# A w_out stage of Winograd type: block sums formed by transfers into DRAM, one load a piece, products one at a time

## The chip, the cores and the metric

The kernel runs on one core of a Trainium2 chip. The metric is the device time of one execution in microseconds (us); given is the median of several runs. Engines are named as in the profile: PE (TensorE matmul), PEld (its weight loads), DVE (VectorE), ACT (ScalarE), POOL (GpSimd), SP (SyncE, which here issues most transfers).

## The reference

One layer on x of 512 tokens by 2048 channels, in float32. The part around the change:

```python
h = rmsnorm(x, g_pre[i])
proj = h @ w_in[i]
...
y_a = o_a @ w_br_a[i]            # branch A: gated DeltaNet
...
y_b = u @ w_br_b[i]              # branch B: convolution, layernorm, swish
gate_a, gate_b = jnp.split(jax.nn.sigmoid(gate_logits + b_gate[i]), N_BRANCHES, axis=-1)
mixed = (gate_a * y_a + gate_b * y_b) @ w_out[i]
x = x + rmsnorm(mixed, g_post[i])
e = p[i] @ w_ple_proj[i]
x = x + rmsnorm(jax.nn.sigmoid(x @ w_ple_gate[i]) * e, g_ple[i])
```

w_out is 2048 by 2048.

## The kernel before

**Precision.** Every large product runs in three passes: each operand is split into a rounded high part and the rest (a cast on ACT, a subtraction on DVE), and three matmuls add high·high, high·low and low·high.

**The stages ahead.** `gemm_cm` makes 128 output channels by 512 tokens from 48 matmuls; its weight tiles of 512 KB are loaded by SP (L122) and split by ACT L127 and DVE L128. It writes one of two PSUM banks of the pool `gps`. After each matmul `tick()` is called: generators that were put in by `spawn(gen, period)` go one step each `period` ticks, so side work is strewn between the matmuls in program order. Branch A's output product (`w_br_a`), the gates (`gate_a`, activation L716), and branch B's convolution (`dwconv`, DVE L689, POOL L693 and L695) interleave so. Branch B's product comes last; its evacuation is DVE L840 (times the gate) and L842 (added to `mixed`). `split_mixed` then makes the operands of the w_out stage out of `mixed`: quadrant A11, the sums S1 to S4, and A12, A22 (L872 to L890; splits by ACT L856 and DVE L858).

**The w_out stage.** The product of two 2 × 2 block matrices is done with seven block products in place of eight, once for each half `jp` of the output columns. With T1 = b11 + b12, T2 = T1 + b22, T3 = b12 + b22 and T4 = T2 + b21 (signs are in the stored blocks), the seven are P1 (A11 by b11), P2 (A12 by b21), P3 (S4 by b22), Q5 (S1 by T1), P6 (S2 by T2), P7 (S3 by T3) and Q4 (A22 by T4). Each product goes over four pieces `q`; a piece is one [128, 1024] block of w_out or of a sum, split by ACT L1037 and DVE L1038 into `wsp` tiles and used by twelve matmuls (L1061 to L1063) into two PSUM banks of 512 columns. That makes 7 × 4 × 2 = 56 pieces.

**Where pieces come from, before.** A table of entries (`e_a`, `e_b`, `e_c`, `e_63`, ...) says which blocks a piece needs. `load` (L978) has three `raw` buffers and, for each fourth load, one buffer `rw`. T1 is formed by a DVE add of two loaded blocks into a tile `t` (L993, four tiles). T2 and T4 are formed by accumulating transfers issued on POOL (`acc`, L985) into the same tile, T3 by a DVE add in place (L1002). So an entry holds one or two loads, an add or an accumulation, and one to three pieces. `next_piece_sw` keeps three or four pieces split ahead of PE and at most two sources loaded ahead of the split.

**Order and banks.** `run(products)` goes through q and, inside, through its products, so products run in pairs or threes: (P1, Q5), (P6, P7, P3), (P2, Q4) for the first half, and (P1, Q5), (P6, P3), (P2), (P7), (Q4) for the second. While the first runs, `stepper` calls the rest of `split_mixed` and `split_s3`. The pool `gps` is closed ahead of the stage and `fps` takes all eight PSUM banks. The products' sums and squares, and x reloaded from DRAM (`xr`, L1127, on SP), make x1; `post` scales it (L1134) by the row factors (`inv_rms`, DVE L957 and L958, POOL L960) and transposes it on PE (L1140). `gemm_tm` with w_ple_gate follows (L1219 to L1221), its weights again by L122, L127 and L128. SP, DVE, ACT and POOL each work off their instructions in order; the compiler's scheduling fixed that order.

Of the kernel before, what the change touches and what calls it, by code (L numbers as in the profile page):

```python
# [82 lines left out]
def _body(ctx, tc, A, out):  # L83
# [636 lines left out]
    def gate_a(i):  # L720
        gemm_cm(w_in_tile(GATE_TILE0 + i), hT, evac_gate(mixed, i, i))
# [205 lines left out]
    run_jobs()  # L927
    lnp_ctx.close()
    s2_ctx.close()
    gps_ctx.close()  # L930

# [4 lines left out]


    s3 = ctx.enter_context(tc.tile_pool(name="s3", bufs=20))  # L940
    fps = ctx.enter_context(tc.tile_pool(name="fps", bufs=8, space=PSUM))
    fsm = ctx.enter_context(tc.tile_pool(name="fsm", bufs=1))
    LOW, HIGH, ALL = (0, 1), (2, 3), (0, 1, 2, 3)
    SLOT, HP_, S3_ = (slots, "s"), (hpool, "h"), (s3, "s3")
# [16 lines left out]
        return r  # L961


    WO = A["w_out"]
    B11, B12, B22, B21 = range(4)
    entries = deque()
    sources = deque()
    pieces = deque()
    tb = {}
    count = [0]  # L970

    def load(jp, blk, q):
        loads[0] += 1
        if early[0] or loads[0] % 4:
            raw = rawp.tile([P, 1024], F32, tag="raw", name="raw", bufs=3)
        else:
            raw = s3.tile([P, 1024], F32, tag="rw", name="rw", bufs=1)
        nc.sync.dma_start(raw, WO[jp, blk, q])  # L978
        return raw

    early = [True]
    loads = [0]

    def acc(t, jp, blk, q):
        nc.gpsimd.dma_start(t, WO[jp, blk, q], accum_op=ALU.add)  # L985

    def e_a(jp, q):
        early[0] = jp == 0
        b11 = load(jp, B11, q)
        b12 = load(jp, B12, q)  # L990
        early[0] = False
        t = tb[q] = s3.tile([P, 1024], F32, tag="t", name="t", bufs=4)
        nc.vector.tensor_tensor(t, b11, b12, ALU.add)  # L993
        return [b11, t]

    def e_63(jp, q):
        acc(tb[q], jp, B22, q)
        return [tb[q], load(jp, B22, q)]

    def sum_t3(jp, q, b22):  # L1000
        b12 = load(jp, B12, q)
        nc.vector.tensor_tensor(b12, b12, b22, ALU.add)  # L1002
        return b12

    def e_b(jp, q):
        acc(tb[q], jp, B22, q)
        b22 = load(jp, B22, q)
        return [tb[q], sum_t3(jp, q, b22), b22]

    def e_p7(jp, q):  # L1010
        return [sum_t3(jp, q, load(jp, B22, q))]

    def e_p2(jp, q):
        acc(tb[q], jp, B21, q)
        return [load(jp, B21, q)]

    def e_t(jp, q):
        return [tb[q]]

    def e_c(jp, q):  # L1020
        return e_p2(jp, q) + [tb[q]]
# [27 lines left out]
    OPND = {"P1": "A11", "Q5": "S1", "P7": "S3", "P6": "S2", "P3": "S4", "P2": "A12", "Q4": "A22"}  # L1049

    def stage(entry, jp):
        for q in range(4):
            entries.append(lambda q=q: entry(jp, q))

    def mms(ps, pr, piece, q, t):
        wh, wl = piece
        for n in range(2):
# [4 lines left out]
            mm(ps, lh, wl[:, c], start=False, stop=False)  # L1062
            mm(ps, ll, wh[:, c], start=False, stop=kk == 7)  # L1063

    def bank():
        return fps.tile([P, T], F32, tag="f", name="f")

    def run(products, side=None):
        ps = {}
        for q in range(4):  # L1070
            for pr in products:
                piece = next_piece_sw()
                if q == 0:
                    ps[pr] = [bank() for _ in range(2)]
                for t in range(2):
# [54 lines left out]
    def post(tts, xr):  # L1130
        rm = inv_rms(ssm[:, tts[0]:tts[0] + 2, :], f"m{tts[0]}")
        for j in range(4):
            for n, tt in enumerate(tts):
                nc.vector.scalar_tensor_tensor(x1[tt][j], x1[tt][j], rm[:, n:n + 1], xr.pop((tt, j)), ALU.mult, ALU.add)  # L1134
            yield
            for k2 in (2 * j, 2 * j + 1):
                ps = fps.tile([P, T], F32, tag="f", name="x1t")
                for n in range(4):
                    k = 2 * k2 + n // 2
                    nc.tensor.transpose(ps[:, n * P:(n + 1) * P], x1[tts[n % 2]][j][:, (k % 4) * P:(k % 4 + 1) * P], ident)  # L1140
                xh = unit(HP_, "xh", F32R)
                nc.scalar.copy(xh, ps)
                xl = unit(HP_, "xl", F32R)
                nc.vector.tensor_tensor(xl, ps, xh.bitcast(F32), ALU.subtract)
                x1T[k2, tts[0] // 2] = (xh, xl)
                yield

    def stepper(gen, n=1):
        def f(k=None):
            for _ in range(n):  # L1150
                next(gen, None)
        return f
# [2 lines left out]
        for _ in gen:  # L1155
            pass

    for e, jp in ((e_a, 0), (e_b, 0), (e_c, 0), (e_a, 1), (e_63, 1), (e_p2, 1), (e_p7, 1), (e_t, 1)):
        stage(e, jp)
# [9 lines left out]
    s5 = [snap(S3_, x) for x in ps["Q5"]]  # L1169
    gp = [bcast_row(A["g_post"], j) for j in (0, 1)]  # L1170
    fin = out_fin(0, gp)
    ps = run(("P6", "P7", "P3"))
    u2 = [add(unit(S3_, "u2"), ps["P6"][t], s1[t]) for t in range(2)]
    d = [minus(unit(S3_, "d"), s5[t], u2[t]) for t in range(2)]
    u3 = [add(u2[t], ps["P7"][t], u2[t]) for t in range(2)]
    for t in range(2):
        fin(t, 1, add(d[t], ps["P3"][t], d[t]))
        fin(2 + t, 1, minus(s5[t], s5[t], u3[t]))
    ps = run(("P2", "Q4"))
    for t in range(2):  # L1180
# [185 lines left out]
```

## Time and profile before

| | |
|---|---|
| median of 3 runs | 2506.57 us (2505.82 to 2507.11) |
| profiled execution | 2508.75 us, span 2507.0 us |
| granted PE clock over the span | 0.998 |
| branch A's output product with gates and convolution | about 985 to 1480 us |
| w_out stage, first matmul to x1's last transposes | about 2144 to 2330 us |
| HBM read, written | 262.66 MB, 14.68 MB |

All times of the profile are from the start of the span of that one execution. "Busy" is the time in which an engine executes instructions; a bracket behind an instruction gives the idle time before it and what ended it. A window row gives busy time and number of instructions for each engine, the granted clock, the share of the 16 DMA engines and the rate. Line numbers in the profile are those of the code printed above; in the new kernel the lines of the stage lie a little elsewhere.

### The profile page before, as it was taken

What the parts mean: (1) busy time and instruction counts of PE and PEld (TensorE: products, weight loads), DVE (VectorE), ACT (ScalarE), POOL (GpSimd) and SP (SyncE); (2) the same over time, 40 slices, a digit from 0 to 9 for tenths busy, and PEclk for the clock granted to TensorE, in tenths of its full rate; (3) what the DMA queues carried; (4) which work ended last, traced back from release to release, by engine and by line L of the source; (5) the groups of instructions that cost most, each with busy time, mean ns of one, the idle gap of its engine ahead of it and who ended that gap; (6) DMA issues with size and microseconds to landing.
All of it is one profiled execution on the core that took longest, in us unless ns stands there. A gap on an engine that the chain in (4) does not pass through costs nothing.

```text
span 2507.0 us, 32580 instructions
## 1 busy us (share of the span) xinstructions
PE 2475.4 (99%) x12202; PEld 2040.6 (81%) x12202; DVE 1654.4 (66%) x3092; ACT 1053.9 (42%) x2083; POOL 134.6 (5%) x151
## 2 busy tenths in 40 slices
PE   8999999999999999999999999999999999998998
PEld 7888888888888888888888888888888888786886
DVE  6776767767676766887877869947323336667644
ACT  6555555565645555322222222235322224444532
POOL 0100000010000000000000000011000000100000
PEclk9999999999999999999999999999999999999999
DMA  6322222222122222323232333422222222676542
GB/s 257 117 96 72 85 80 85 81 76 89 67 92 79 84 85 76 109 97 109 97 109 97 102 105 110 165 87 101 101 96 97 98 96 99 190 228 197 200 170 76
DMA packets 85406, 279.45 MB, mean 111 GB/s; under 512 B 9472, under 2 KB 9728, under 8 KB 85248
## 3 DMA queue, kind: packets, MB, share of 16 engines
q1 hardware_dynamic: 81792, 266.89, 30.6%
q0 software_dynamic: 2304, 8.39, 1.8%
q10 hardware_dynamic: 1152, 2.10, 0.3%
q8 instruction: 95, 1.56, 0.2%
q14 instruction: 63, 0.52, 0.1%
HBM read 262.66 MB, written 14.68 MB: 111 GB/s over the span
## 4 chain that ended last, share of the span: by engine, by line
PE 94%; DMA 2%; DVE 2%; issue 1%; ACT 1%; POOL 0%; SPq 0%; DVEq 0%; POOLq 0%; ACTq 0%
PE g L184 25%; PE g L186 25%; PE g L182 25%; PE f L1221 2%; PE f L1219 2%; PE f L1220 2%; DMA raw<-in_w_out 1%; PE psB L468 1%; PE f L1062 1%; PE f L1063 1%; PE f L1061 1%; PE psS L474 1%; PE psA L462 1%; PE pg L569 1%; PE f L1296 0%
## 5 line engine op out<-in xcount | busy, mean ns | idle before, releaser
L186 PE MATMUL g<-hh,w 128*128 128x512 f32 x2320 | 916.0, 395 | 1.6 <-DVE w L128 1.6
L184 PE MATMUL g<-hl,w 128*128 128x512 f32 x2320 | 916.6, 395 | 0.0
L182 PE MATMUL g<-hh,w 128*128 128x512 f32 x2320 | 913.8, 394 | 0.0
L127 ACT CAST w<-raw 128x512 fp32r<-128x512 f32 x780 | 478.1, 619 | 867.1 <-PE g L186 760.0
L128 DVE TENSOR_TENSOR w<-raw,w 128x512 fp32r<-128x512 f32 x780 | 551.2, 711 | 433.4 <-ACT w L127 431.3
L186 PEld LDWEIGHTS g<-hh,w 128*128 128x128 f32 x2320 | 436.6, 188 | 88.7 <-DVE w L128 4.7
L184 PEld LDWEIGHTS g<-hl,w 128*128 128x128 f32 x2320 | 436.4, 188 | 86.2 <-issue 1.6
L182 PEld LDWEIGHTS g<-hh,w 128*128 128x128 f32 x2320 | 436.7, 188 | 84.2 <-issue 0.2
L689 DVE SCALAR_TENSOR_TENSOR uc<-sg,vec,uc 128x511 f32<-128x511 f32 (+14 forms) x480 | 351.3, 734 | 14.0 <-ACT uc L686 3.9
L410 DVE SCALAR_TENSOR_TENSOR cv<-g,vec,cv 128x511 f32<-128x511 f32 x144 | 106.3, 738 | 31.2 <-ACT cv L408 30.9
L184 PE MATMUL g<-ul,w 128*128 128x512 f32 x256 | 99.7, 390 | 0.0
L184 PE MATMUL g<-ol,w 128*128 128x512 f32 x256 | 99.7, 390 | 0.0
L186 PE MATMUL g<-oh,w 128*128 128x512 f32 x256 | 99.7, 389 | 0.0
L182 PE MATMUL g<-oh,w 128*128 128x512 f32 x256 | 99.7, 389 | 0.0
L182 PE MATMUL g<-uh,w 128*128 128x512 f32 x256 | 99.7, 389 | 0.0
L186 PE MATMUL g<-uh,w 128*128 128x512 f32 x256 | 99.7, 389 | 0.0
L604 DVE TENSOR_TENSOR prod<-UT,VT 128x2 f32<-128x2 f32 (+30 forms) x248 | 87.1, 351 | 6.6
L1061 PE MATMUL f<-wsp,oph 128*128 128x512 f32 x192 | 76.3, 401 | 6.2 <-ACT wsp L1037 6.1
L1062 PE MATMUL f<-wsp,oph 128*128 128x512 f32 x192 | 76.9, 401 | 2.7 <-DVE wsp L1038 2.6
L1220 PE MATMUL f<-w,xh 128*128 128x512 f32 x192 | 75.0, 391 | 2.1 <-DVE w L128 1.9
L1063 PE MATMUL f<-wsp,opl 128*128 128x512 f32 x192 | 75.6, 395 | 0.0
L1221 PE MATMUL f<-w,xl 128*128 128x512 f32 x192 | 75.0, 391 | 0.0
(298 smaller groups left out, 2666.5 us busy)
## 6 DMA issues: line engine op xcount, KB each, us to landing
raw<-in_w_in SPq DMA_DIRECT2D x290, 512.0 KB, 3.2
raw<-in_w_ple_gate SPq DMA_DIRECT2D x40, 512.0 KB, 4.2
raw<-in_w_out SPq DMA_DIRECT2D x35, 512.0 KB, 5.4
raw<-in_w_br_a SPq DMA_DIRECT2D x32, 512.0 KB, 3.3
raw<-in_w_br_b SPq DMA_DIRECT2D x32, 512.0 KB, 3.2
t<-in_w_out POOLq DMA_DIRECT2D x16, 512.0 KB, 8.3
rw<-in_w_out SPq DMA_DIRECT2D x9, 512.0 KB, 4.7
x<-in_x SPq DMA_DIRECT2D x8, 512.0 KB, 9.4
```

Of the source, the lines that this page charges most:

```text
L127: nc.scalar.copy(hi, rq)
L128: nc.vector.tensor_tensor(lo, rq, hi.bitcast(F32), ALU.subtract)
L182: mm(ps, wh, rh, start=(k == 0), stop=False)
L184: mm(ps, wh, rl, start=False, stop=False)
L186: mm(ps, wl, rh, start=False, stop=(k == NK - 1))
L410: nc.vector.scalar_tensor_tensor(y[:, s:], ps[:, 0:T - s], vv(w0 + 3 - s), y[:, s:], ALU.mult, ALU.add)
L689: nc.vector.scalar_tensor_tensor(y[:, s:], u[:, 0:T - s], vv(w0 + TAPS - 1 - s), y[:, s:], ALU.mult, ALU.add)
L1061: mm(ps, lh, wh[:, c], start=kk == 0, stop=False)
L1062: mm(ps, lh, wl[:, c], start=False, stop=False)
L1063: mm(ps, ll, wh[:, c], start=False, stop=kk == 7)
L1220: mm(ps[tt], lh, wl, start=False, stop=False)
L1221: mm(ps[tt], ll, wh, start=False, stop=k == NK - 1)
```

## The change

1. A generator `presum` is put in after `finish("oa")` in branch A, with a period of ten ticks. For each of the eight (jp, q) it has POOL issue 20 transfers of [128, 512] (256 KB): four plain loads and eight accumulating loads of w_out blocks into four tiles of the pool `slots`, and eight stores that put T1, T3, T2 and T4 into a DRAM tensor `wo_sums`. Ahead of the stores of T2 and of T4 it waits 24 ticks. That is 160 transfers, 42 MB. The four tiles come out of the tiles that gates and convolution use too.
2. In the stage every piece is one load by SP (now L1015), from w_out or from `wo_sums`. The DVE adds L993 and L1002 and the accumulating transfers L985 are gone. There are three `raw` and five `rw` buffers, in a cycle of eight loads (the first three loads take `raw`); up to five sources are loaded ahead of the split, and each split is followed by one more load.
3. Products run one at a time: P1, P2, Q5, P6, P3, P7, Q4 for the first half, P1, Q5, P6, P3, P2, P7, Q4 for the second. The side work during the first P1 goes four steps a piece in place of two.
4. `gps` stays open; `fps` has six banks, and `bank()` takes them in turn with the two of `gps`. x1's transposes take their bank there too.

```diff
-    gps_ctx = ExitStack()
-    gps = gps_ctx.enter_context(tc.tile_pool(name="gps", bufs=2, space=PSUM, side="right"))
+    gps = ctx.enter_context(tc.tile_pool(name="gps", bufs=2, space=PSUM, side="right"))
...
+    sums = dram.tile([2, 4, 4, P, 1024], F32, name="wo_sums")
+
+    def presum():
+        for jp in range(2):
+            for q in range(4):
+                cs = [slice(n * T, n * T + T) for n in range(2)]
+                a = [slots.tile([P, T], F32, tag="s", name="wsum") for n in range(2)]
+
+                def take(t, blk, add):
+                    for n in range(2):
+                        nc.gpsimd.dma_start(t[n], WO[jp, blk, q][:, cs[n]], **(dict(accum_op=ALU.add) if add else {}))
+                        yield
+
+                def give(t, m):
+                    for n in range(2):
+                        nc.gpsimd.dma_start(sums[jp, m, q][:, cs[n]], t[n])
+                        yield
+                yield from take(a, B11, False)
+                b = [slots.tile([P, T], F32, tag="s", name="wsum") for n in range(2)]
+                yield from take(b, B12, False)
+                yield from take(a, B12, True)
+                yield from take(b, B22, True)
+                yield from give(a, T1)
+                yield from give(b, T3)
+                yield from take(a, B22, True)
+                yield 24
+                yield from give(a, T2)
+                yield from take(a, B21, True)
+                yield 24
+                yield from give(a, T4)
+
     jobs.append(lambda: finish("oa"))
+    jobs.append(lambda: spawn(presum(), 10, "presum"))
...
-    gps_ctx.close()
...
-    fps = ctx.enter_context(tc.tile_pool(name="fps", bufs=8, space=PSUM))
+    fps = ctx.enter_context(tc.tile_pool(name="fps", bufs=6, space=PSUM))
...
+    WHICH = {"P1": (WO, B11), "P2": (WO, B21), "P3": (WO, B22),
+             "Q5": (sums, T1), "P6": (sums, T2), "P7": (sums, T3), "Q4": (sums, T4)}
-    def load(jp, blk, q):
+    def load(jp, pr, q):
+        n = loads[0]
         loads[0] += 1
-        if early[0] or loads[0] % 4:
+        if n < 3 or n % 8 in (1, 4, 7):
             raw = rawp.tile([P, 1024], F32, tag="raw", name="raw", bufs=3)
         else:
-            raw = s3.tile([P, 1024], F32, tag="rw", name="rw", bufs=1)
+            raw = s3.tile([P, 1024], F32, tag="rw", name="rw", bufs=5)
...
     def next_piece_sw():
-        ahead = 3 if count[0] < 10 else 4
-        while len(pieces) < ahead and (sources or entries):
-            while len(sources) < 2 and entries:
-                sources.extend(entries.popleft()())
+        while len(sources) < 5 and entries:
+            load(*entries.popleft())
+        while len(pieces) < (3 if count[0] < 10 else 4) and sources:
             split_piece()
+            if entries:
+                load(*entries.popleft())
         return pieces.popleft()
...
     gen = opening()
-    ps = run(("P1", "Q5"), stepper(gen, 2))
+    ps = run(("P1",), stepper(gen, 4))
     drain(gen)
...
+    ps = run(("P2",))
+    for t in range(2):
+        fin(t, 0, add(unit(S3_, "c11"), ps["P2"][t], s1[t]))
+    ps = run(("Q5",))
```

**How the order moves, first place: SP at the opening of the stage.** Rows are SP's transfers in its order; raw and rw are buffers, their numbers tell the tiles apart. Before:

```order
L978 DMA raw_17493<-in_w_out 128x1024
L978 DMA raw_17495<-in_w_out 128x1024
L978 DMA raw_17503<-in_w_out 128x1024
L978 DMA rw_17725<-in_w_out 128x1024
L978 DMA raw_17505<-in_w_out 128x1024
L978 DMA raw_17538<-in_w_out 128x1024
L978 DMA raw_17540<-in_w_out 128x1024
```

Now (pieces 0, 1, 2, 4, 7, 3, 5, 6 and 8):

```order
L1015 DMA raw_17685<-in_w_out 128x1024
L1015 DMA raw_17687<-in_w_out 128x1024
L1015 DMA raw_17689<-in_w_out 128x1024
L1015 DMA raw_17693<-in_w_out 128x1024
L1015 DMA raw_17711<-in_w_out 128x1024
L1015 DMA rw_17691<-in_w_out 128x1024
L1015 DMA rw_17699<-in_w_out 128x1024
L1015 DMA rw_17705<-in_w_out 128x1024
L1015 DMA rw_17750<-wo_sums_9445 128x1024
```

Five loads into raw tiles now stand ahead of the first rw load, in place of three; four rw loads follow it, where before raw loads did. raw_17711 takes the tile of raw_17687 and waits for that one's split.

**Second place: DVE at the opening.** gt are the gated outputs of branch B, sf and opl the stage's operands, wsp the split pieces. Before:

```order
L1038 TENSOR_TENSOR wsp_17500<-raw_17493,wsp_17499 128x1024
L840 TENSOR_TENSOR gt_16964<-g_17418,gt_16964 128x512
L842 TENSOR_TENSOR gt_12906<-gt_12906,gt_16964 128x512
L993 TENSOR_TENSOR t_17497<-raw_17493,raw_17495 128x1024
L1038 TENSOR_TENSOR wsp_17514<-raw_17503,wsp_17513 128x1024
L872 TENSOR_TENSOR sf_17362<-gt_10506,gt_12906 128x256
L1038 TENSOR_TENSOR wsp_17510<-t_17497,wsp_17509 128x1024
L858 TENSOR_TENSOR opl_17536<-sf_17362,oph_17534 128x512
L858 TENSOR_TENSOR opl_17626<-sf_17079,oph_17624 128x512
L993 TENSOR_TENSOR t_17507<-raw_17503,raw_17505 128x1024
```

Now (the last gate operation is L877, the split L1033; ahead of these rows stand, in this order, the split of piece 0, L875 and the split of piece 1):

```order
L877 TENSOR_TENSOR gt_13099<-gt_13099,gt_17157 128x512
L907 TENSOR_TENSOR sf_17555<-gt_10553,gt_13099 128x256
L1033 TENSOR_TENSOR wsp_17708<-raw_17689,wsp_17707 128x1024
L893 TENSOR_TENSOR opl_17732<-sf_17555,oph_17730 128x512
L893 TENSOR_TENSOR opl_17778<-sf_17272,oph_17776 128x512
L918 TENSOR_TENSOR sf_17555<-sf_17555,gt_10239 128x256
L918 TENSOR_TENSOR sf_17555<-sf_17555,gt_10553 128x256
L921 TENSOR_TENSOR sf_17735<-gt_12787,sf_17555 128x256
L921 TENSOR_TENSOR sf_17735<-gt_13099,sf_17555 128x256
L893 TENSOR_TENSOR opl_17770<-gt_12787,oph_17768 128x512
L893 TENSOR_TENSOR opl_17744<-sf_17555,oph_17742 128x512
L1033 TENSOR_TENSOR wsp_17747<-rw_17691,wsp_17746 128x1024
```

The sums L993 are gone, and the subtraction of piece 3 (wsp_17747) comes after those of pieces 1 and 2 and after the operand work.

**Third place: SP where x is loaded again, in the second half.** xr are the x tiles. Before:

```order
L1127 DMA xr_18302<-in_x 128x512
L978 DMA raw_18221<-in_w_out 128x1024
L1127 DMA xr_18304<-in_x 128x512
L1127 DMA xr_18306<-in_x 128x512
L978 DMA raw_18256<-in_w_out 128x1024
L1127 DMA xr_18308<-in_x 128x512
```

Now:

```order
L1122 DMA xr_18492<-in_x 128x512
L1122 DMA xr_18494<-in_x 128x512
L1122 DMA xr_18496<-in_x 128x512
L1015 DMA rw_18418<-in_w_out 128x1024
L1015 DMA raw_18438<-in_w_out 128x1024
L1122 DMA xr_18498<-in_x 128x512
L1122 DMA xr_18500<-in_x 128x512
```

The eight x loads stand in groups of two and three with two w_out loads between, in place of one w_out load each.

More of the change, by code (lines that the diff above doesn't have):

```diff
@@ L752, in evac_ya @@
         return f
+    WO = A["w_out"]
+    B11, B12, B22, B21 = range(4)
+    T1, T2, T3, T4 = range(4)
+    sums = dram.tile([2, 4, 4, P, 1024], F32, name="wo_sums")
[25 more added lines that the diff above has]
+                yield from give(a, T4)
     gate_a(4)
@@ L961, in inv_rms @@
         return r
-    WO = A["w_out"]
-    B11, B12, B22, B21 = range(4)
+    OPND = {"P1": "A11", "Q5": "S1", "P7": "S3", "P6": "S2", "P3": "S4", "P2": "A12", "Q4": "A22"}
+    WHICH = {"P1": (WO, B11), "P2": (WO, B21), "P3": (WO, B22),
+             "Q5": (sums, T1), "P6": (sums, T2), "P7": (sums, T3), "Q4": (sums, T4)}
     entries = deque()
@@ L968, in _body @@
     pieces = deque()
-    tb = {}
     count = [0]
-    def load(jp, blk, q):
+    loads = [0]
+    def load(jp, pr, q):
+        n = loads[0]
         loads[0] += 1
-        if early[0] or loads[0] % 4:
+        if n < 3 or n % 8 in (1, 4, 7):
             raw = rawp.tile([P, 1024], F32, tag="raw", name="raw", bufs=3)
         else:
-            raw = s3.tile([P, 1024], F32, tag="rw", name="rw", bufs=1)
[L978 to L1021, printed above, removed]
+            raw = s3.tile([P, 1024], F32, tag="rw", name="rw", bufs=5)
+        src, blk = WHICH[pr]
+        nc.sync.dma_start(raw, src[jp, blk, q])
+        sources.append(raw)
     def split_piece():
@@ L1063, in mms @@
             mm(ps, ll, wh[:, c], start=False, stop=kk == 7)
+    banks = [0]
     def bank():
-        return fps.tile([P, T], F32, tag="f", name="f")
+        banks[0] += 1
+        if banks[0] % 8 < 6:
+            return fps.tile([P, T], F32, tag="f", name="f")
+        return gps.tile([P, T], F32, tag="g", name="f")
     def run(products, side=None):
@@ L1136, in post @@
             for k2 in (2 * j, 2 * j + 1):
-                ps = fps.tile([P, T], F32, tag="f", name="x1t")
+                ps = bank()
                 for n in range(4):
@@ L1156, in drain @@
             pass
-    for e, jp in ((e_a, 0), (e_b, 0), (e_c, 0), (e_a, 1), (e_63, 1), (e_p2, 1), (e_p7, 1), (e_t, 1)):
-        stage(e, jp)
+    for jp, prs in ((0, ("P1", "P2", "Q5", "P6", "P3", "P7", "Q4")), (1, ("P1", "Q5", "P6", "P3", "P2", "P7", "Q4"))):
+        entries.extend((jp, pr, q) for pr in prs for q in range(4))
     def opening():
@@ L1165, in _body @@
     gen = opening()
-    ps = run(("P1", "Q5"), stepper(gen, 2))
+    ps = run(("P1",), stepper(gen, 4))
     drain(gen)
     s1 = [snap(S3_, x) for x in ps["P1"]]
-    s5 = [snap(S3_, x) for x in ps["Q5"]]
     gp = [bcast_row(A["g_post"], j) for j in (0, 1)]
     fin = out_fin(0, gp)
-    ps = run(("P6", "P7", "P3"))
-    u2 = [add(unit(S3_, "u2"), ps["P6"][t], s1[t]) for t in range(2)]
+    ps = run(("P2",))
+    for t in range(2):
+        fin(t, 0, add(unit(S3_, "c11"), ps["P2"][t], s1[t]))
+    ps = run(("Q5",))
+    s5 = [snap(S3_, x) for x in ps["Q5"]]
+    ps = run(("P6",))
+    u2 = [add(s1[t], ps["P6"][t], s1[t]) for t in range(2)]
     d = [minus(unit(S3_, "d"), s5[t], u2[t]) for t in range(2)]
+    ps = run(("P3",))
+    for t in range(2):
+        fin(t, 1, add(d[t], ps["P3"][t], d[t]))
+    ps = run(("P7",))
     u3 = [add(u2[t], ps["P7"][t], u2[t]) for t in range(2)]
     for t in range(2):
-        fin(t, 1, add(d[t], ps["P3"][t], d[t]))
         fin(2 + t, 1, minus(s5[t], s5[t], u3[t]))
-    ps = run(("P2", "Q4"))
-    for t in range(2):
-        fin(t, 0, add(s1[t], ps["P2"][t], s1[t]))
+    ps = run(("Q4",))
     for t in range(2):
         fin(2 + t, 0, add(u3[t], ps["Q4"][t], u3[t]))
-    ps = run(("P1", "Q5"))
+    ps = run(("P1",))
     s1 = [snap(SLOT, x) for x in ps["P1"]]
-    s5 = [snap(SLOT, x) for x in ps["Q5"]]
     gp = [bcast_row(A["g_post"], j) for j in (2, 3)]
     fin = out_fin(1, gp)
+    ps = run(("Q5",))
+    s5 = [snap(SLOT, x) for x in ps["Q5"]]
     xr = load_x_again(LOW, HP_)
-    ps = run(("P6", "P3"))
+    ps = run(("P6",))
     u2 = [add(unit(SLOT, "u2"), ps["P6"][t], s1[t]) for t in range(2)]
+    d = [minus(unit(SLOT, "d"), s5[t], u2[t]) for t in range(2)]
+    ps = run(("P3",))
     for t in range(2):
-        d = minus(unit(SLOT, "d"), s5[t], u2[t])
-        fin(t, 1, add(d, ps["P3"][t], d))
+        fin(t, 1, add(d[t], ps["P3"][t], d[t]))
     ps = run(("P2",))
@@ L1240, in hold @@
         if k < 14:
-            pool, tag, bufs = (s3, "t", 4) if k < 4 else (s3, "rw", 1) if k < 5 else (s3, "wx", 5) if k < 10 else (ring, "w", 4)
+            pool, tag, bufs = (s3, "rw", 5) if k < 5 else (s3, "wx", 5) if k < 10 else (ring, "w", 4)
             w = pool.tile([P, 1024], F32R, tag=tag, name="wh", bufs=bufs)
```

6 lines of the change are left out of this document (1 added, 5 removed).

## The prediction

> **What bounds the kernel now.** The page's first part says which engine to watch.
>
> ```profile
> PE 2475.4 (99%) x12202; PEld 2040.6 (81%) x12202; DVE 1654.4 (66%) x3092; ACT 1053.9 (42%) x2083; POOL 134.6 (5%) x151
> ```
>
> TensorE is busy for 2475.4 of 2507.0 us of span, and the change leaves the number of matmuls alone. So it can win only idle time of PE and time at a lower clock, and can lose only by making PE wait. Next, the busy time by windows: branch A, where the transfers are added, and then those 10 us windows of the w_out stage in which PE isn't full. Columns: window, its length, PE, PEld, DVE, ACT and POOL busy, the granted clock, the DMA share, GB/s.
>
> ```profile
> 985.00:1480.00 495.00, 495.00 (x2185) 410.14 (x2184) 396.94 (x580) 143.38 (x233) 14.04 (x11) 1.00 0.30 103
> 2140.00:2150.00 10.00, 9.12 (x41) 7.28 (x40) 6.26 (x8) 4.19 (x6) 0.33 (x1) 1.00 0.33 115
> 2150.00:2160.00 10.00, 8.74 (x37) 6.42 (x35) 7.47 (x12) 3.71 (x5) 1.60 (x2) 1.00 0.97 249
> 2160.00:2170.00 10.00, 7.17 (x29) 5.13 (x29) 8.00 (x10) 5.20 (x8) 1.75 (x2) 1.00 0.87 257
> 2260.00:2270.00 10.00, 8.07 (x28) 6.06 (x27) 6.20 (x6) 5.26 (x6) 1.74 (x2) 0.83 0.60 141
> 2280.00:2290.00 10.00, 9.58 (x42) 7.36 (x40) 6.89 (x9) 3.33 (x7) 0.00 (x0) 1.00 0.89 310
> 2290.00:2300.00 10.00, 7.25 (x33) 5.47 (x34) 8.38 (x12) 5.43 (x7) 0.73 (x1) 1.00 0.93 319
> 2310.00:2320.00 10.00, 8.07 (x44) 6.44 (x42) 9.55 (x17) 4.66 (x11) 0.00 (x0) 1.00 0.04 15
> 2320.00:2330.00 10.00, 9.44 (x48) 7.20 (x47) 9.38 (x18) 5.00 (x10) 1.20 (x1) 1.00 0.69 227
> 2330.00:2340.00 10.00, 10.00 (x53) 8.32 (x53) 9.43 (x16) 5.77 (x11) 0.00 (x0) 1.00 0.93 332
> ```
>
> Ten minus the PE column is the loss: 0.88 + 1.26 + 2.83 = 4.97 us at the opening, 1.93 in the 2260s, 0.42 + 2.75 = 3.17 in 2280:2300, 1.93 + 0.56 = 2.49 at the end of the last product. Together 12.56 us. The last row is a control: 332 GB/s, and PE is full. The waits of PE over the stage say for whom it stood still.
>
> ```profile
> PE f L1061 <- ACT wsp L1037: 6.1, 5, 1.5
> PE f L1062 <- DVE wsp L1038: 2.6, 3, 1.2
> PE f L1220 <- DVE w L128: 1.9, 1, 1.9
> PE x1t L1140 <- DVE snap L1134: 0.4, 1, 0.4
> ```
>
> 8.7 us are waits for the split of a w_out piece. The chain of waits says what the splits waited for:
>
> ```profile
> 2146.41 4.71 DMA raw<-in_w_out
> 2151.15 1.24 DVE t L993
> 2152.44 5.67 DMA raw<-in_w_out
> ```
>
> A load, then a DVE sum that alone frees the buffer, then the next load: a loop over three buffers. The change cuts it.
>
> There is a second loss in the 2260s, where the clock reads 0.83. PE's timeline:
>
> ```profile
> 2261.42 0.50 PE L1061 MATMUL f<-wsp,oph 128*128 128x512 f32 x1 [1.17 <-ACT wsp L1037]
> 2262.68 0.50 PE L1062 MATMUL f<-wsp,oph 128*128 128x512 f32 x1 [0.76 <-DVE wsp L1038]
> 2263.94 0.63 PE L1061 MATMUL f<-wsp,oph 128*128 128x512 f32 x1
> 2267.35 0.40 PE L1063 MATMUL f<-wsp,opl 128*128 128x512 f32 x1
> ```
>
> Between the last two starts lie eight matmuls in 3.41 us. The normal pitch comes from the gates of branch A, whose activations follow two gemms of 48 matmuls:
>
> ```profile
> 1213.94 0.69 ACT L716 ACTIVATE gt<-g,vec 128x512 f32<-128x512 f32 x1 [2.10 <-PE g L186]
> 1224.82 0.60 ACT L679 ACTIVATE sg<-g 128x512 f32<-128x512 f32 x1 [2.10 <-PE g L186]
> ```
>
> 10.88 us over 48 is 0.2267 us. Eight are 1.81 us, so 1.60 us went to the clock, and all that can be won is 12.56 + 1.60 = 14.2 us. A piece (12 matmuls) lasts 2.72 us.
>
> **The change part by part.** *The stage's sums.* Eight L993 and eight L1002 adds of about 1.23 us leave DVE (20 us), sixteen accumulating transfers leave Pool, and each piece needs one load. Buffers go from 3 + 1 to 3 + 5, each used again after eight loads, that is 8 × 2.72 = 21.8 us. Against that stand:
>
> ```profile
> raw<-in_w_out SPq DMA_DIRECT2D x35, 512.0 KB, 5.4
> t<-in_w_out POOLq DMA_DIRECT2D x16, 512.0 KB, 8.3
> ```
>
> A load of 5.4 us and a split of some 2.3 us fit in that more than twice, so past the opening I cost the loads at nothing; were that cover gone, the old waits (1.2 to 1.5 us each) would be back. The 3.17 us of 2280:2300 go, but for the 0.4 us of the first transposes (<- DVE snap), whose code is kept: gain 2.8. The 1.93 us in the 2260s go too. There SP also stood in line for the x tiles:
>
> ```profile
> 2234.25 2.52 SPq L1127 DMA_DIRECT2D xr<-in_x  x3
> 2243.07 21.09 SPq L978 DMA_DIRECT2D raw<-in_w_out  x4
> ```
>
> In the new order these x loads still block w_out loads behind them, but with five loads ahead and tiles freed by a P1 that runs alone. With the stall I let its 1.60 us of clock go: gain 3.5. That is a choice: 2160:2170 and 2290:2300 show more idle time at clock 1.00.
>
> The Trainium skill, "TensorE: Matmul & The Clock Gate", Part 1, has the clock fall only after an idle window of about 3.4 us. This trace shows it fall after 1.17 and 0.76 us with one matmul between, so the measurement decides; by the page the 1.60 us would have another cause and could stay, and the time would be 1.6 us higher than my forecast.
>
> *The opening.* The two g banks stay, so the first matmul need not wait for L840: 0.88 goes. Pieces 0, 1, 2 and 4 are loaded before the stage. Piece 3 is the late one. Its buffer is in a pool that opens when the last gate is done:
>
> ```profile
> 2143.67 0.69 DVE L840 TENSOR_TENSOR gt<-g,gt 128x512 f32<-128x512 f32 x1 [4.16 <-PE g L186]
> 2146.26 1.22 DVE L1038 TENSOR_TENSOR wsp<-raw,wsp 128x1024 fp32r<-128x1024 f32 x1
> 2147.40 0.42 DVE L872 TENSOR_TENSOR sf<-gt 128x256 f32<-128x256 f32 x1
> 2148.87 1.28 DVE L858 TENSOR_TENSOR opl<-sf,oph 128x512 fp32r<-128x512 f32 x2
> 2145.17 0.33 SPq L978 DMA_DIRECT2D rw<-in_w_out  x1
> ```
>
> Before, the first rw load left at 2145.17. In the new order the load of piece 7 stands ahead and waits for the split of piece 1, so piece 3's leaves near 2146.2. PE wants it at 2143.5 + 3 × 2.72 = 2151.6, and its second matmul, which needs the subtraction, at 2151.9. On DVE stand before that subtraction two gate operations, two splits, five half-width operations and two pairs of opl: 2 × 0.69 + 2 × 1.22 + 5 × 0.42 + 2 × 1.28 = 8.5 us from 2143.67, so it ends at 2152.2 + 1.2 = 2153.4 if the load (4.71 us, as in the first chain row) is there in time: a wait of 1.5 us. With the 5.67 us of the third row it lands at 2151.9, and cast and subtraction, at 1.22 each, end at 2154.3: 2.4 us. I take 2.0. Piece 8's subtraction stands behind the L1082 add that needs the last matmul of P2's first half: 0.69 + 1.22 against the second half's six matmuls (1.36) is a wait of 0.5 us. The opening thus goes from 4.97 to 2.5: gain 2.5.
>
> *The tail.* The last product's end keeps its form:
>
> ```profile
> 2318.68 0.50 PE L1220 MATMUL f<-w,xh 128*128 128x512 f32 x1 [1.93 <-DVE w L128]
> ```
>
> The first window row of the end has DVE at 9.55 of 10, and the new code gives it the same operations after the last matmul (unscaled sums, squares, x1), with PE fed by the same weight splits. Bounds are 0 and 2.49 us; I take it as nearly kept, 2.3: gain 0.2.
>
> *The transfers in branch A.* 160 Pool transfers of 256 KB. A step each 10 matmuls, eight iterations of about 248 matmuls: 8 × 56.2 = 450 us, done some 700 us before the stage. PE is full there, so there is nothing to win, only to lose. The queues:
>
> ```profile
> q1 hardware_dynamic: 81792, 266.89, 30.6%
> q0 software_dynamic: 2304, 8.39, 1.8%
> L127 ACT CAST w<-raw 128x512 fp32r<-128x512 f32 x780 | 478.1, 619 | 867.1 <-PE g L186 760.0
> ```
>
> 266.89 MB in 30.6% of 2507 us is 348 GB/s at full share, 8.39 MB in 1.8% is 186 GB/s. An iteration (12 plain or storing, 8 accumulating) then takes 9.0 + 11.3 = 20.3 us of 56.2: share 0.30 + 0.36 = 0.66, below the 0.93 that left PE full. The weight casts L127 waited 760.0 us for PE's buffers and hardly for loads. On Pool, adds queue behind a transfer that waits up to 8.3 us:
>
> ```profile
> 1396.56 1.29 POOL L695 TENSOR_TENSOR acc<-acc,uc 128x512 f32<-128x512 f32 x1 [42.24 <-DVE uc L689]
> ```
>
> Pool stood idle 42.24 us before this one; nothing late arises. I cost this part at 0.
>
> **Sum.** 2.8 + 3.5 + 2.5 + 0.2 = 9.0 us. The profiled execution is 2508.75 us (span 2507.0 and 1.75 around it), 2.2 above the median 2506.57; 2508.75 − 9.0 = 2499.75 for a profiled run, 2506.57 − 9.0 = **2497.6** as a median.
>
> **The rivals.** *A: the burst of loads at the opening is late.* Some seven loads leave within 2 us; they may share the queues instead of coming in order. If piece 3 takes 8.3 us like a t transfer, it lands at 2154.5, its cast and subtraction end at 2156.9, PE loses 5.0 us instead of 2.0, and the clock may drop as in the 2260s (1.6). Gain 9.0 − 3.0 − 1.6 = 4.4: 2502.2. For it: 1.26 and 2.83 us of idle time at DMA shares of 0.97 and 0.87. Against: those loads came one after the other, behind a sum.
>
> *B: slower, DVE becomes the bound in branch A.* DVE is busy 396.94 of 495 us, so over 450 us it has 89 us free. If a Pool transfer's issue shuts DVE out while it lasts, 160 × 0.87 = 139 us come on top, 50 more than there is, and PE waits for splits: 2497.6 + 50 = 2547.6. It decides from 89 / 160 = 0.56 us of DVE lost for each transfer. The rows:
>
> ```profile
> 2155.16 0.87 POOL L985 DMA_DIRECT2D t<-in_w_out  x1 [4.43 <-DVE wsp L1038]
> 2155.37 1.22 DVE L1038 TENSOR_TENSOR wsp<-raw,wsp 128x1024 fp32r<-128x1024 f32 x1
> ```
>
> The subtraction beside an issue took 1.22 us, as long as the one at 2146.26 without. That speaks against, on one pair.
>
> The Trainium skill, "SBUF — State Buffer", section "Who interferes with whom", names an exclusive lock between DVE and GpSimd; there a DVE operation with two SBUF inputs contends only with a GpSimd instruction that reads SBUF. This pair agrees so far.
>
> *C: the freed time is filled again.* New waits (piece 8, the x loads that block SP, a queue of wo_sums loads) add up to what is won: 2506.6, no change. For it: idle time in this stage has sat at changing places, each with its own last waiter. Against: eight buffers and 20 us less DVE work.
>
> **How the numbers follow.** About 0.2% (5 us) can be told from no change: faster is under 2501.6, slower over 2511.6. I give my case 0.60, A 0.20, C 0.12, B 0.08. My case's own bounds: all 14.2 us won is 2492.4; piece 3 at 2.4 us, the 1.6 of clock kept and nothing from the tail is 2499.8; all of it is faster. A lies 0.6 us past the border: 0.08 of it counts as faster, 0.12 as same. Faster 0.60 + 0.08 = 0.68, same 0.12 + 0.12 = 0.24, slower 0.08. The range goes from 2493 to 2505: my case but its last half microsecond, and A with as much again on its slow side; it leaves out B and C.
>
> **What would show it.** Right: no accumulating transfer in the stage, PE full in 2160:2170 of its new place and from there to the transposes, one wait of 1.5 to 2.4 us on piece 3's subtraction, about 2.3 us at the last product's end, clock 1.00, and branch A of equal length. A: PE's largest wait is on ACT's cast of piece 3, with a load of over 7 us ahead of it in the chain. B: DVE's mean times in branch A longer, and PE's first idle time there. C: waits for splits that again sum to 8 us, on other pieces. The forecast is wrong in kind if branch A is longer by over 1 us.

## The result and the profile after

The changed kernel takes 2490.76 us (median of 4 runs, 2490.61 to 2492.22) against 2506.84 us before (4 runs, 2505.82 to 2508.05): 16.1 us less, ratio 0.9937 with a 95% interval of 0.992 to 0.9954. The profiled execution went from 2508.75 (span 2507.0) to 2490.88 us (span 2489.1). The direction was forecast; the gain is 16 us in place of 9, and the time lies 2.2 us under the range.

First the waits of PE in the changed kernel from 2130 us on:

```profile
PE f L1135 <- DVE snap L1129: 0.7, 1, 0.7
PE f L1052 <- DVE wsp L1033: 0.7, 1, 0.7
PE f L1135 <- DVE c L1129: 0.6, 1, 0.6
PE f L1051 <- ACT wsp L1032: 0.2, 1, 0.2
```

Of 12.3 us of waits 2.2 are left: 0.9 on the split of one piece and 1.3 on transposes (L1135). The waits for the gate's evacuation and for the first w_ple_gate weights (1.9) are gone. Where the splits were late, the windows now read:

```profile
2140.00:2150.00 10.00, 9.32 (x40) 7.06 (x38) 8.80 (x14) 5.95 (x10) 0.00 (x0) 1.00 0.66 235
2150.00:2160.00 10.00, 9.78 (x43) 8.12 (x44) 10.00 (x12) 7.69 (x11) 0.00 (x0) 1.00 0.95 328
2160.00:2170.00 10.00, 9.90 (x44) 7.84 (x43) 6.75 (x9) 5.72 (x9) 0.00 (x0) 1.00 0.88 331
2260.00:2270.00 10.00, 10.00 (x46) 8.17 (x45) 7.35 (x8) 5.48 (x8) 0.00 (x0) 1.00 0.86 292
2290.00:2300.00 10.00, 10.00 (x57) 8.45 (x56) 9.55 (x17) 4.97 (x10) 0.00 (x0) 1.00 0.32 104
```

Nowhere in the stage does the clock column fall, and PE is full at a DMA share of 0.86. Branch A, with the transfers in it:

```profile
985.00:1480.00 495.00, 495.00 (x2186) 409.87 (x2185) 396.76 (x578) 141.63 (x231) 124.33 (x171) 1.00 0.66 188
```

PE is still full there, DVE busy 396.76 us as before, POOL 124 us in place of 14, and the DMA share is the 0.66 of the forecast.

By place, from the starts of matmuls in both traces: the w_out stage (from the last matmul of branch B's product, so with the wait between, to the last of the stage) went from 172.65 to 160.19 us, which is 12.5; from the first matmul behind the stage to the last of the kernel 181.27 became 178.81, 2.5. Within the stage, comparing matmuls of the same number, the gain is 4.9 us at the opening, 4.0 in the 2260s and 3.5 behind them. A further 3.2 us of the difference between the two profiled executions lie ahead of branch A. The first gate there, before, after, and in a second profile of the kernel before (c_before, below):

```profile
996.34 0.69 ACT L716 ACTIVATE gt<-g,vec 128x512 f32<-128x512 f32 x1 [1.54 <-PE g L186]
```

```profile
993.08 0.69 ACT L715 ACTIVATE gt<-g,vec 128x512 f32<-128x512 f32 x1 [1.53 <-PE g L185]
```

```profile
994.02 0.69 ACT L716 ACTIVATE gt<-g,vec 128x512 f32<-128x512 f32 x1 [1.54 <-PE g L186]
```

The unchanged kernel stands at 996.34 once and at 994.02 once, and two kernels below that share its code up to there (e8 and e11) stand at 993.35 and 993.17, so this belongs to single executions. In the slower start the first x tiles land some 2 us later, PE waits 0.6 and 1.0 us near 13 us and then has a stretch of low clock. It is no part of the change.

### The profile page after: what moved, and what is told of

It is laid out like the page before. It is cut to its first block, busy times and chain, and to the rows that moved or that the text cites. A ratio compares the mean times of both kernels' runs of the same rounds, so it can differ in the third digit from the quotient of the medians.

```text
span 2489.1 us, 32807 instructions
## 1 busy us (share of the span) xinstructions
PE 2469.3 (99%) x12202; PEld 2037.7 (82%) x12202; DVE 1639.5 (66%) x3076; ACT 1055.6 (42%) x2083; POOL 230.8 (9%) x295
## 3 DMA queue, kind: packets, MB, share of 16 engines
q0 software_dynamic: 16896, 41.95, 6.9%
## 4 chain that ended last, share of the span: by engine, by line
PE 97%; DVE 1%; issue 1%; ACT 0%; POOL 0%; DMA 0%; SPq 0%; DVEq 0%; POOLq 0%; ACTq 0%
PE g L183 26%; PE g L185 26%; PE g L181 25%; PE f L1052 2%; PE f L1053 2%; PE f L1051 2%; PE f L1223 2%; PE f L1222 2%; PE f L1221 2%; PE psB L467 1%; PE psS L473 1%; PE psA L461 1%; PE pg L568 1%; PE f L1300 0%; PE f L1298 0%
## 5 line engine op out<-in xcount | busy, mean ns | idle before, releaser
L767 POOL DMA_DIRECT2D wsum<-in_w_out x96 | 75.2, 839 | 72.1 <-issue 22.3
```

## The experiments

Theory 1: all of the gain lies in the stage and the start of the product behind it, and the transfers in branch A cost nothing. Its parts: (a, c) the loop of two loads, a DVE sum and a split on few buffers kept the splits late; (b) the depth of the buffers. Rivals: (2) the transfers cost something; (3) running products one at a time is what helps; (4) the accumulating transfers filled the DMA queues. Each ratio below is against the kernel before on the same chip.

**The transfers alone (e1).** The kernel before, with this and `presum` as in the change:

```diff
     jobs.append(lambda: finish("oa"))
+    jobs.append(lambda: spawn(presum(), 10, "presum"))
```

> The kernel before with the 160 Pool transfers of the change added in branch A, whose sums nobody reads. Theory 1 (all the gain lies in the w_out stage and its tail; the transfers cost nothing): 2506.8 us as before, within 1 us, and the gates of branch A 43.52 us apart as before. Theory 2 (the transfers cost something that the stage's gain hides, through DVE or the DMA queues): 2 to 50 us slower, with the gates of branch A further apart.

Measured 2507.79 us, ratio 1.0006 (0.9997 to 1.0015). The gates of branch A are 43.52 us apart, as before. The window of branch A:

```profile
985.00:1480.00 495.00, 495.00 (x2186) 409.87 (x2185) 396.86 (x579) 142.80 (x232) 124.73 (x171) 1.00 0.66 188
```

**The change without the transfers (e2).**

```diff
-    jobs.append(lambda: spawn(presum(), 10, "presum"))
-             "Q5": (sums, T1), "P6": (sums, T2), "P7": (sums, T3), "Q4": (sums, T4)}
+             "Q5": (WO, B12), "P6": (WO, B22), "P7": (WO, B12), "Q4": (WO, B21)}
```

> The changed kernel without the transfers; in place of the four sums the stage loads single blocks of w_out, so the block sums are left out of the computation. Theory 1: 2490.8 us like the changed kernel, within 1 us. Theory 2: faster than the changed kernel by what the transfers cost, 2 us or more.

Measured 2491.39 us, ratio 0.9939 (0.9925 to 0.9952), no faster than with them. From both sides, the 160 transfers cost nothing that can be measured, and theory 2 falls.

**The transfers denser (e7).** A step each three matmuls in place of ten:

```diff
-    jobs.append(lambda: spawn(presum(), 10, "presum"))
+    jobs.append(lambda: spawn(presum(), 3, "presum"))
```

> The changed kernel with the transfers of branch A three times as dense (a step each 3 matmuls in place of 10), so that they ask for about 0.9 of the DMA engines' time on top of the 0.30 of the weight loads, for some 190 us. If only the DMA queues' room kept them free of cost, weight loads now come late and PE waits in branch A: 2493 to 2520 us, with DMA shares near 1 there. If Pool's issuing held DVE, DVE's operations there would take longer. If the buffers ahead cover even this: 2490.8 us.

Measured 2490.69 us, ratio 0.9934 (0.9921 to 0.9948): again no cost. But the transfers did not come three times as densely: the 160 were issued over 287 us, where the change takes 428, so about 1.5 times. The window of the dense stretch, and then the convolution's DVE operations in it (busy, mean ns), for this kernel and for the change:

```profile
985.00:1200.00 215.00, 215.00 (x950) 178.16 (x949) 178.22 (x264) 66.24 (x109) 89.27 (x127) 1.00 0.90 250
```

```profile
L688 DVE SCALAR_TENSOR_TENSOR uc<-sg,vec,uc 128x511 f32<-128x511 f32 (+11 forms) x160 | 118.4, 746 | 3.9 <-ACT uc L685 1.0
```

```profile
L688 DVE SCALAR_TENSOR_TENSOR uc<-sg,vec,uc 128x504 f32<-128x504 f32 (+13 forms) x160 | 116.5, 734 | 3.9 <-ACT uc L685 1.0
```

At a DMA share of 0.90 over 215 us PE is full, so the weight buffers of branch A cover even that. The waits that I feared don't begin there; a share nearer to 1 was not reached.

**Before's four buffers (e3).**

```diff
-        if n < 3 or n % 8 in (1, 4, 7):
+        if n < 8 or n % 4 != 3:
-            raw = s3.tile([P, 1024], F32, tag="rw", name="rw", bufs=5)
+            raw = s3.tile([P, 1024], F32, tag="rw", name="rw", bufs=1)
...
-        while len(sources) < 5 and entries:
+            while len(sources) < 2 and entries:
...
```

The rest of the edit puts the reading-ahead loop back to that of before, and gives the last weights of w_ple_gate, used long after the stage, the tiles that they had before.

> The changed kernel with the load buffers of before: three raw and one rw, two sources ahead in place of eight buffers and five sources. Theory 1a (the DVE sum in the loop of load, sum, split was the cause): a buffer comes round each 4 pieces, 10.9 us, against 5.4 us of load and 2.3 of split, so only the opening suffers: 2491 to 2494 us. Theory 1b (the depth of the loads was the cause): the waits for splits come back, 8 us in sum with 0.3 for each on top: 2500 to 2504 us.

Measured 2492.71 us, ratio 0.9947 (0.9934 to 0.9959): 2 us slower than the change. Its waits:

```profile
PE f L1049 <- ACT wsp L1032: 2.9, 1, 2.9
PE f L1050 <- DVE wsp L1033: 0.7, 1, 0.7
PE f L1133 <- DVE snap L1127: 0.7, 1, 0.7
PE f L1133 <- DVE c L1127: 0.6, 1, 0.6
```

One wait of the opening grows to 2.9 us, behind a load of 7.48 us in its chain:

```profile
2156.03 7.48 DMA raw<-wo_sums
```

The profiled execution took 2495.11 us, 2.4 more than the median, and has a stretch of low clock in the stage, so it shows the kind of loss and not its usual size. The four extra buffers are worth some 2 of the 16 us; theory 1b, as the main cause, falls.

**Before's pairs of products (e4).** Loads, sums and banks as changed, the products, and what is done with them, in the groups of before:

```diff
-    for jp, prs in ((0, ("P1", "P2", "Q5", "P6", "P3", "P7", "Q4")), (1, ("P1", "Q5", "P6", "P3", "P2", "P7", "Q4"))):
-        entries.extend((jp, pr, q) for pr in prs for q in range(4))
+    for jp, groups in ((0, (("P1", "Q5"), ("P6", "P7", "P3"), ("P2", "Q4"))),
+                       (1, (("P1", "Q5"), ("P6", "P3"), ("P2",), ("P7",), ("Q4",)))):
+        for prs in groups:
+            entries.extend((jp, pr, q) for q in range(4) for pr in prs)
...
```

> The changed kernel with the products in the pairs and threes of before: (P1, Q5), (P6, P7, P3), (P2, Q4) and so on; loads, sums and banks as changed. Theory 1a: the loads don't care in which order pieces are used: 2491 to 2494 us. Rival 3 (running the products singly is what spreads DVE's sums, squares and transposes and takes the waits away): 2497 us or more, with PE's waits at the ends of the groups.

Measured 2491.02 us, ratio 0.9937 (0.9925 to 0.995): with the new loads the order of the products is worth nothing, and rival 3 falls.

**The DVE adds put back (e5).** In `split_piece`, with the product's name beside each source:

```diff
+        if pr in ("Q5", "P7"):
+            nc.vector.tensor_tensor(src, src, src, ALU.add)
```

> The changed kernel with a DVE add of 1.2 us put back ahead of the split of each Q5 and P7 piece (16 adds of the loaded block to itself, so these blocks enter doubled); loads, buffers and transfers as changed. Theory 1a in the form that the waits came from DVE's time for the sums: the waits for splits return, 6 us or more: 2497 to 2502 us. Theory 1c (they came from the loop of two loads and a sum on few buffers, not from DVE's time): each piece still has its block early, 2491 to 2493 us.

Measured 2491.44 us, ratio 0.9937 (0.9924 to 0.9949). The adds are there, 16 of them at 1.22 us:

```profile
L1021 DVE TENSOR_TENSOR rw<-rw 128x1024 f32<-128x1024 f32 x11 | 13.3, 1223 | 4.0 <-DMA rw<-wo_sums 4.0
L1021 DVE TENSOR_TENSOR raw<-raw 128x1024 f32<-128x1024 f32 x5 | 6.1, 1223 | 1.0 <-DMA raw<-wo_sums 1.0
```

So 20 us of DVE time in the stage cost nothing as long as an add needs one block that was loaded early. What cost time before was, by this, not DVE's work of adding, but what the adds waited for and held.

**The wide banks closed (e6).**

```diff
-    fps = ctx.enter_context(tc.tile_pool(name="fps", bufs=6, space=PSUM))
+    gps_ctx.close()
+    fps = ctx.enter_context(tc.tile_pool(name="fps", bufs=8, space=PSUM))
```

> The changed kernel with the pool of the two wide banks closed ahead of the stage and eight banks given to the stage's pool, as before. If the wait of the first matmul on the last gate's evacuation (0.88 us of idle time) costs its idle time and about 0.25 us of restart: 1.1 us slower than the changed kernel, about 2492, with that wait back in the trace. If the split of piece 3 is late anyway and sets the end of the opening: no change, 2490.8, the 0.9 us of waits for piece 3 gone in exchange.

Measured 2491.85 us, ratio 0.9939 (0.9927 to 0.9951), 1.1 us slower than the change, as the first case said; its runs (from 2491.13) overlap those of the change. In the trace, where it can be told, the stage lasts 161.77 us, 1.6 more, and the wait is back:

```profile
PE f L1053 <- ACT wsp L1034: 0.9, 1, 0.9
PE f L1053 <- DVE gt L876: 0.9, 1, 0.9
```

**The sums taken away one by one.** Three kernels are the kernel before plus the transfers (which e1 shows to be free), with one kind of sum taken from DRAM. T1 (e8):

```diff
-        b12 = load(jp, B12, q)
-        nc.vector.tensor_tensor(t, b11, b12, ALU.add)
+        nc.sync.dma_start(t, sums[jp, T1, q])
```

> The kernel before, with the transfers in branch A, whose T1 is loaded from DRAM into the t tile in place of a second load and the DVE add; T3 is still added on DVE, T2 and T4 still accumulated by Pool transfers. Theory 1c: the opening's waits fall (some 4 us of its 6.4 with restarts), the later ones stay: 2501 to 2504 us. If the accumulating transfers or the depth of four buffers were the cause instead: 2506 to 2508 us, the waits where they were.

Measured 2500.66 us, ratio 0.9976 (0.9967 to 0.9985): a gain of 6.5 us, a little more than theory 1c said. The largest waits:

```profile
PE f L1094 <- DVE wsp L1070: 3.3, 3, 2.6
PE f L1252 <- DVE w L128: 2.1, 2, 2.0
PE f L1093 <- DVE gt L875: 0.9, 1, 0.9
PE f L1093 <- ACT wsp L1069: 0.8, 1, 0.8
```

The number of loads is the same as before (the sum's load replaces that of b12). But two things went together: the add that joined two loads, and one of the two loads that took one of the four raw and rw buffers, since the sum now lands in a tile t. This run does not part them. The wait near 2261 went as well, which I had not expected, though the DMA share from 2220 to 2260 us is 0.95 here.

T3 (e9):

```diff
-        b12 = load(jp, B12, q)
-        nc.vector.tensor_tensor(b12, b12, b22, ALU.add)
-        return b12
+        return load(jp, T3, q, sums)
```

> The kernel before, with the transfers in branch A, whose T3 is loaded from DRAM (no second load, no add in place); T1 is still added on DVE, T2 and T4 still accumulated by Pool transfers. Theory 1c: the waits at about 2261, 2291 and 2298 us go with the clock's drop (4.1 and some 3 us), the opening's stay: 2499 to 2502 us. If the accumulating transfers were their cause: 2505 to 2508 us.

Measured 2505.42 us, ratio 0.9993 (0.9984 to 1.0002): not what was expected. The waits for splits behind 2290 us went, those at 2259 us (1.17 and 0.76) stayed, and a new, longer wait came. The largest:

```profile
PE x1t L1171 <- DVE snap L1165: 5.8, 1, 5.8
PE f L1092 <- ACT wsp L1068: 3.6, 5, 1.2
PE f L1093 <- DVE wsp L1069: 1.6, 3, 0.8
```

Transposes now stand in PE's order ahead of matmuls whose pieces were ready, and wait 5.75 us for x1. The wait for w_ple_gate's first weights (1.9) is gone in this kernel.

T2 and T4 (e11), with no accumulating transfer left in the stage:

```diff
-        acc(tb[q], jp, B22, q)
-        return [tb[q], load(jp, B22, q)]
+        return [load(jp, T2, q, sums), load(jp, B22, q)]
...
-        return e_p2(jp, q) + [tb[q]]
+        return e_p2(jp, q) + [load(jp, T4, q, sums)]
```

> The kernel before, with the transfers in branch A, whose T2 and T4 are loaded from DRAM; the sixteen accumulating transfers of the stage are gone, the DVE sums T1 and T3 stay. Theory 4 (the waits at about 2261 us and 2291 to 2298 us come from DMA queues that the accumulating transfers fill: share 0.93 from 2220 to 2260, loads that take 11 us and more): those waits and the clock's drop go, the opening's stay: 2499 to 2502 us. Theory 1c (the loop of loads and DVE sums on four buffers alone): no change or slower, 2505 to 2509 us, since T2 and T4 now take their turn in the four buffers too.

Measured 2500.8 us, ratio 0.9976 (0.9965 to 0.9987): 6.9 us. That is what theory 4 said, and not theory 1c, so the accumulating transfers were part of the cause. The windows from 2220, here and, behind it, in the kernel before:

```profile
2220.00:2260.00 40.00, 40.00 (x176) 32.84 (x175) 26.49 (x27) 20.93 (x28) 0.00 (x0) 1.00 0.77 263
```

```profile
2220.00:2260.00 40.00, 40.00 (x177) 32.78 (x175) 22.49 (x23) 15.28 (x23) 5.21 (x6) 1.00 0.93 259
```

At the same rate the DMA share falls from 0.93 to 0.77, a w_out load into a raw buffer lands after 4.0 us (median) in place of 10.0, and the wait at 2261 is gone. It went with T1's sums too (e8), at a share of 0.95. So it needed both: queues near full, and a sum that waits for two loads on four buffers. Not all that theory 4 said came: a wait of 1.96 us stays at 2289, and the clock falls there and at the opening.

T1 and T3 (e10), the edits of e8 and e9 together:

```diff
-        nc.vector.tensor_tensor(t, b11, b12, ALU.add)
+        nc.sync.dma_start(t, sums[jp, T1, q])
...
-        return [sum_t3(jp, q, load(jp, B22, q))]
+        return [sum_t3(jp, q, None)]
```

> The kernel before, with the transfers in branch A, whose T1 and T3 are both loaded from DRAM, with no DVE sum left in the stage; T2 and T4 are still accumulated by Pool transfers. Theory 1c: all waits for splits but some 3 us at the opening go: 2494 to 2498 us. Theory 4: the accumulating transfers keep the DMA queues full from 2220 to 2260 us and part of the later waits stays: 2498 to 2502 us.

Measured 2496.69 us, ratio 0.9961 (0.9948 to 0.9973): 11.0 us between the medians (9.8 by the ratio), as theory 1c said. All waits for splits that its profile shows are at the opening, 5.1 us, of which one is 4.1; that execution took 2499.94 us, 3.2 more than the median. The gains of e10 and e11 add up to more than the whole, so the two causes overlap and have no separate shares. The last 5 us of the change are left for the accumulating transfers, the four buffers more (e3: 2) and the banks (e6: 1); they were not split further.

**The kernel before once more (c_before),** with no edit:

> The kernel before, unchanged, for a second profile. The first profile loses 3.2 us against the changed kernel's within its first 20 us, in code that the change doesn't touch. If that loss belongs to single executions: up to 3.2 us less here, with the stage's waits as in the first profile; if it belongs to the kernel, it is here again.

Its span is 2506.4 us, and 2.3 us of the start's 3.2 are gone, but the stage took 174.37 us in place of 172.65. Its windows:

```profile
2150.00:2160.00 10.00, 6.97 (x28) 4.84 (x28) 7.06 (x11) 5.07 (x7) 0.87 (x1) 0.99 0.95 240
2160.00:2170.00 10.00, 10.00 (x37) 7.74 (x36) 7.27 (x8) 4.38 (x7) 1.74 (x2) 0.84 0.92 252
2260.00:2270.00 10.00, 8.71 (x30) 6.72 (x31) 7.08 (x6) 4.38 (x5) 1.73 (x2) 0.83 0.68 153
```

There are two stretches of low clock in the stage, in place of one. In e1, the same stage, it took 175.11 us, with two and a third right behind it. The stalls and the clock's drops change from one execution to the next; the profile on which I forecast held the shortest stage of the three.

## Why the prediction was right or wrong

**Right: what bounds the kernel, and where the gain lies.** PE's waits for splits, from loads that a sum held up. e8, e10 and e11 show that taking the sums away gives the gain back in parts, e5 that it is not DVE's time. What the account did not hold is the part of the accumulating transfers: they made the loads themselves late (e11).

**Right: the transfers in branch A at 0.** The share of 0.66 was met to the digit; e1, e2 and e7 bound the cost from both sides. Rival B falls: the lock would have had to take 0.56 us of DVE for each transfer, and DVE's busy time is unchanged within 0.2 us over 171 POOL instructions.

**Wrong: the sum of 9.0 us, and the bound above it, "all that can be won is 12.56 + 1.60 = 14.2 us".** The kernel won 16.1. In the two profiles the terms of the sum, in its order, came to 3.5 us (2280:2300, forecast 2.8), 4.0 (the 2260s, 3.5), 4.9 (the opening, 2.5) and 2.5 (the tail, 0.2), 14.9 in all. Most of the miss is thus the opening and the tail, both treated below. In the bound two things failed. The first is that I took idle time for lost time. A stall of the kernel before, in PE's timeline:

```profile
2164.91 0.39 PE L1063 MATMUL f<-wsp,opl 128*128 128x512 f32 x1
2166.77 0.50 PE L1061 MATMUL f<-wsp,oph 128*128 128x512 f32 x1 [1.48 <-ACT wsp L1037]
2167.11 0.40 PE L1062 MATMUL f<-wsp,ah 128*128 128x512 f32 x1
2167.35 0.40 PE L1063 MATMUL f<-wsp,al 128*128 128x512 f32 x1
```

From the first to the last start lie 2.44 us for three matmuls, which at the pitch of 0.2267 take 0.68: 1.76 us are lost where the bracket says 1.48. Matmuls overlap (0.39 us each at that pitch), and the idle time begins only when the last of them has ended; the restart then is slower too (0.34 us to the next start). Over the whole stage the same shows: its length, less its idle time and 1.7 us for the stretch of low clock (3.41 us at a granted clock of 0.5), is 161.0 us before and 158.7 after, with seven waits fewer. That is 0.3 us for each. Seven fewer waits in the stage and one behind it are thus, as an estimate, 2.2 to 2.6 us that I had not counted.

The second is that the sum was tied to one execution. The three profiles of that stage lasted 172.65, 174.37 and 175.11 us, mean 174.04, against 160.19 after: a gain of 13.9 in the stage, and with 2.5 behind it 16.3, which is the 16.1 of the medians. The matching sum of that one profile is the 14.9 above.

**Mis-sized: the opening.** Forecast was a gain of 2.5 us, from 4.97 to 2.5. The working for piece 3 held: it was worked out to be ready at 2153.4, which is 2150.2 in the new trace with its start 3.2 us earlier, and there the second row's matmul, which needs it, begins:

```profile
2148.81 0.73 PE L1051 MATMUL f<-wsp,ah 128*128 128x512 f32 x2 [0.23 <-ACT wsp L1032]
2150.22 0.50 PE L1052 MATMUL f<-wsp,ah 128*128 128x512 f32 x1 [0.68 <-DVE wsp L1033]
```

Start to start that loses 1.5 us, the lower of my bounds; I chose 2.0. The wait for piece 8's subtraction came as well, too short to be listed as a wait:

```profile
2163.49 0.61 PE L1051 MATMUL f<-wsp,oph 128*128 128x512 f32 x2
2164.21 0.50 PE L1052 MATMUL f<-wsp,oph 128*128 128x512 f32 x1
```

With the slower restart behind it about 0.4 us are lost there, where 0.5 was forecast. So the new opening loses 1.9 us in place of the 2.5 of the forecast. The larger error is on the other side: from start to start the old opening lost 6.8 us, not its 4.97 us of idle time, for the reason above.

**Right in kind: the 2260s and 2280:2300.** Both are gone, with the clock's drop, and the 0.6 us of the first transposes stayed near the 0.4 that I kept. Letting the 1.60 us of clock go was right: in three profiles of the stage before, such a drop came once or twice, and in the changed kernel and in e2, e4, e5, e6 and e7 never. The Trainium skill, "TensorE: Matmul & The Clock Gate", Part 1, has a window of about 3.4 us, and the drops in this stage last 3.41 us each, or twice that (6.83, in e9 and e10). But the waits ahead of the one here, 1.17 and 0.76 us, are shorter than the page's idle window, while 1.29 and 1.48 us at the opening of the same trace brought none; which waits bring one is not shown.

**Wrong: the tail, "I take it as nearly kept, 2.3: gain 0.2".** It gained 2.5. The step said that the new code gives DVE the same operations after the last matmul. It does, but no longer in the same order. DVE in the new kernel:

```profile
2295.96 1.28 DVE L128 TENSOR_TENSOR w<-raw,w 128x512 fp32r<-128x512 f32 x2
2297.43 1.29 DVE L128 TENSOR_TENSOR w<-raw,w 128x512 fp32r<-128x512 f32 x2 [0.19 <-ACT w L127]
2298.64 1.28 DVE L1139 TENSOR_TENSOR xl<-f,xh 128x512 fp32r<-128x512 f32 x2
2299.84 1.50 DVE L1082 TENSOR_TENSOR u<-f,u 128x512 f32<-128x512 f32 x2
```

Four splits of w_ple_gate now precede the last product's sums (L1082, which wait for its last matmuls); in the kernel before the first of them stood behind the same sums (L1087):

```profile
2316.75 1.28 DVE L1087 TENSOR_TENSOR u<-f,u 128x512 f32<-128x512 f32 x2
2317.95 0.68 DVE L128 TENSOR_TENSOR w<-raw,w 128x512 fp32r<-128x512 f32 x1
```

PE's wait for them, 1.93 us, went with that. I read the order of the two kernels at the opening and not here. It changed in e9 and e10 too, and not in e8 and e11, so taking T3's second load and add away is enough for it. SP also loads w_ple_gate earlier in the new kernel (from 2269.89 us in place of 2291.69), but the time of that load does not decide by itself: in e3 and e8 it begins at 2283.40 and 2283.25, some 21 and 23 us ahead of the stage's end, and e3 has the new order and e8 the old. What moved the order stays open.

**Rivals.** A did not come: piece 3's load landed after 4.1 us, in time, and only those behind it took 6.4 to 9.0 us. Nor did C, though e9 shows that C can happen: there a new wait of 5.75 us ate what the old ones gave back.

## What to carry to other kernels

A sum formed on the spot from two loads costs little as work and much as a meeting point: it holds two buffers until the later load lands, and queues that are nearly full make that later load late (here the work, the buffer and the queues were not priced one by one). Where the operands are weights and an earlier stage has DMA time to spare, form them there and let the tight stage have one independent load for each use. And size a stall from start to start of the instructions around it, over more than one execution, and look at the fixed order at every place where a wait is forecast to stay.

## What the runs showed of the hardware

- 160 Pool transfers of 256 KB, 96 into tiles at 0.84 us of POOL each and 64 stores at 0.61, left DVE as it was at 0.734 us an operation; with the transfers about 1.5 times as dense (e7) it was 0.746.
- PE stayed full over 215 us at a DMA share of 0.90 (e7).
- In the stage before, 3.39 MB of accumulating transfers took 43.9% of the DMA engines' time between 2228 and 2268 us, and 5.98 MB of plain ones 41.1%:

```profile
q0 software_dynamic: 924, 3.39, 43.9%
q1 hardware_dynamic: 2211, 5.98, 41.1%
```

So an accumulated byte cost 1.9 times a loaded one, as over the whole run. It is not POOL's queue alone: in branch A of the change (985 to 1450 us) that queue moved 41.95 MB, 16.8 of them accumulated, in 37.1% of the DMA engines' time; at the prediction's 186 GB/s for every byte it would have been 48%, as an estimate. In the stretch from 2228 to 2268 us of the kernel before, a w_out load took 11.5 us to land.
